# The last gate of a two-layer trunk: half of its K as seven block products instead of eight

## The chip, the cores and the metric

One core of a Trainium2 chip runs the whole program in one launch. The metric is device time in microseconds, of which the median over runs is given. The core has TensorE (PE, matmuls, with PEld its weight loads), VectorE (DVE), ScalarE (ACT), GpSimd (POOL) and SyncE (SP, which issues the DMA transfers of the kernel before). Each engine runs its own queue of instructions in order, and semaphores order them against each other.

## What is computed

A trunk of two layers over 512 tokens of 1024 channels in float32. Each layer has a token mixer, a squared-ReLU MLP, two layer norms, and at its end a gate:

```python
h = layer_norm(DEEPNORM_ALPHA * x + mix, ln_g[i, 0], ln_b[i, 0])
h = layer_norm(DEEPNORM_ALPHA * h + sq_relu_mlp(h, mlp_w1[i], mlp_w2[i]), ln_g[i, 1], ln_b[i, 1])
x = h + jax.nn.sigmoid(h @ ple_w_gate[i]) * (p[i] @ ple_w_proj[i])
```

The change is in the gate of the second layer, the last line at i = 1. There `h` is 512 x 1024, `ple_w_gate` 1024 x 1024, `p` 512 x 256 and `ple_w_proj` 256 x 1024; the result goes to the output.

## The kernel before

A float32 matrix is split into a high part (`hi`, rounded to the matmul's format) and a low part (`lo`, the remainder), and a product is three matmuls, high x high, high x low and low x high (`mm3`, L119). One matmul takes 128 rows of K, 128 tokens and 512 output columns. A weight arrives as a *unit* of 128 partitions x 1024 (two blocks of K by 512 columns, 512 KB): SP loads it into one of three `raw` buffers, ACT casts it to `whi` (L113), DVE subtracts to `wlo` (L116), in six buffers each.

The token dimension has four chunks of 128. The MLP's second matrix is applied in block products (`block_product`, L344), each of which replaces eight products of half blocks by seven with sums of blocks. Its weight sums are made by DVE in eight buffers `r` (`weight_sums`, L320). The last of them, in the order p1, p7, p6, p4, p5, p2, p3, ends with the layer norm: chunks 0 and 1 are normalised after p5, chunks 2 and 3 after p3 (`norm`, L283, `layer_norm`, L199), and each chunk of `acc` is transposed to serve as the stationary side of the gate (`transpose_split`, L231). A chunk has two groups of four transposes (q = 0 for the first half of the channels, q = 1 for the second); a group goes into a PSUM bank `pt`, ACT casts it (L242) and DVE subtracts (L243) into `h_s`.

The gate (L474 to L512) then runs over two halves `h` of the output columns and four chunks `c`: a projection of 6 matmuls (`proj`, L466) and a gate product of 24 matmuls over eight blocks of K (L493) into a PSUM bank `pj`; ACT takes the sigmoid (L496), DVE multiplies with the projection (L503) and adds `acc` (L506), and SP stores. In the first half all four projections come first, so that the transposes of chunks 0 and 1 can stand between them; those of chunks 2 and 3 stand inside the gate products of chunks 0 and 1. The very last projection is done in two halves of 256 columns behind the last gate product.

What sets the order: the program is scheduled by priorities when it is built. `tc.high_priority(offset=...)` moves instructions ahead by so many places (LEAD is 100, SOON 40); `behind(ins)` places one after a given instruction. From then on each engine's queue is fixed.

Of the kernel before, what the change touches and what calls it, by code (L numbers as in the profile page):

```python
# [15 lines left out]
P = 128  # L16
# [28 lines left out]
def trunk(ctx: ExitStack, tc, a):  # L45
# [73 lines left out]
    def mm3(out, sh, sl, mh, ml, start, stop, **kw):  # L119
        nc.tensor.matmul(out, sh, mh, start=start, stop=False, **kw)  # L120
        nc.tensor.matmul(out, sh, ml, start=False, stop=False, **kw)  # L121
        nc.tensor.matmul(out, sl, mh, start=False, stop=stop, **kw)  # L122

    class Split:

# [102 lines left out]
    def behind(ins):  # L228
        return tc.issue_after(ins.ins) if ins is not None else nullcontext()

    def transpose_split(src, dst, c, apart):  # L231

        sl = slice(c * P, (c + 1) * P)
        for q in range(2):
            pt = bank(psm, "pm") if apart and q else bank(pst, "pt")
            for j in range(4):
                k = 4 * q + j
                nc.tensor.transpose(pt[:, j * P : (j + 1) * P], src[:, k * P : (k + 1) * P], ident)  # L238
            v = pt.rearrange("p (j t) -> p j t", j=4)
            h = dst.hi[q][:, :, sl]  # L240
            with tc.high_priority(offset=LEAD if apart else SOON):
                nc.scalar.copy(h, v)  # L242
                turned_last[:] = [nc.vector.tensor_sub(dst.lo[q][:, :, sl], v, f32(h))]  # L243
            yield

    def out_part(units, n, xs, c, h, first, scale, last=False, sums=None):
# [33 lines left out]
                for c in range(NCH):  # L280
                    out_part(units, 4, xs, c, h, first, scale)

    def norm(i):  # L283
# [9 lines left out]
        return h_s, chunk, lambda c: transpose_split(acc[:, c, :], h_s, c, c == 3 and i % 2 == 0), sums  # L293

# [49 lines left out]
    def block_product(w, blk, lead, first, after=None, turns=None, sums=None, low=None):  # L344
# [41 lines left out]
        for f in (p1, p7, p6, p4, p5, p2, p3) if after else (p1, p2, p6, p7, p5, p4, p3):  # L386
# [4 lines left out]
                after(2), after(3)  # L391
            yield

    def mlp_and_gate(layer, h_s, last):

        w1, w2 = a[f"w1_{layer}"], a[f"w2_{layer}"]
# [34 lines left out]
        for g, period in enumerate(PERIODS):  # L431
            if g < 4:
                tiles = hidden(g)
            if g > 0:
                if g == 4:
                    h_s, after, turned, sums = norm(2 * layer + 1)
# [11 lines left out]
        x_n = None if last else Split(8)  # L448
        rows = None if last else [tmp("blk", [P, 2, 4, 256]) for _ in range(2)]
        late = []  # L450

        def turn(h, c):
# [10 lines left out]

        pps = {}

        def proj(c, pu, chunk=None, cs=slice(0, T)):  # L466

            ps = pps[c] = bank(*((psj, "pj") if c > 1 and pps else (psy, "py%d" % (c % 2))))
            sl = slice(c * P, (c + 1) * P) if chunk is None else slice(chunk * P, (chunk + 1) * P)
            for k in range(2):  # L470
                ks = slice(k * 512 + cs.start, k * 512 + cs.stop)
                mm3(ps[:, cs], p_s[0][:, k, sl], p_s[1][:, k, sl], pu[0][:, ks], pu[1][:, ks], k == 0, k == 1)

        for h in range(2):  # L474
            pu = unit(a[f"wp_{layer}"][h])
            gu = [unit(a[f"wg_{layer}"][4 * h + j]) for j in range(4)]
            for c in range(NCH):
                sl = slice(c * P, (c + 1) * P)
                if h == c == 0:
                    turns = turned(1)  # L480
                    for i in range(NCH):
                        proj(i, pu)
                        if i in (1, 2):
                            next(turns)
                end = last and h == 1 and c == NCH - 1
                if h == 1 and not end:
# [7 lines left out]
                    if turns and k in (2, 5):  # L494
                        next(turns)
                nc.scalar.activation(sg, pg, AF.Sigmoid)  # L496
                for i in range(2 if end else 1):
                    n = 256 if end else 512
                    cs = slice(i * n, (i + 1) * n)
                    if end:  # L500
                        proj(i, pu, c, cs)
                    pp = pps.pop(i if end else c)[:, cs]
                    nc.vector.tensor_mul(sg[:, cs], pp, sg[:, cs])  # L503
                    fs = slice(h * 512 + i * n, h * 512 + (i + 1) * n)
                    d = acc[:, c, fs]
                    nc.vector.tensor_add(d, sg[:, cs], d)  # L506
                    if last:
                        nc.sync.dma_start(a["out"][c * P : (c + 1) * P, fs], d)
                while late:
                    late.pop(0)()  # L510
                if not last:
                    late.append(lambda h=h, c=c: turn(h, c))  # L512
        return x_n, rows, late

    def values4(xs, rows, late):
# [791 lines left out]
```

## Time and profile before

| | |
|---|---|
| median of 3 runs | 1414.23 us (1414.07 to 1414.66) |
| the profiled execution | 1415.16 us |
| its span, first to last instruction | 1413.4 us |
| transposes behind the last block product start | 1350.97 us |
| last sigmoid of the gate starts | 1408.05 us |
| last operation of DVE starts | 1410.09 us |

A row of the timeline reads: start in us from the span's start, duration in us, engine, line of the kernel, operation, output<-inputs by the program's names, shapes, count, and in brackets how long the engine idled before it and what ended that. L numbers of profiles of before are lines of the kernel before. A row of a table of stretches has the stretch, its length, busy time (and instructions) of PE, PEld, DVE, ACT and POOL, the granted clock of TensorE as a share of full speed, the DMA engines' busy share and GB/s. The DMA rows end with the median time from issue to landing.

### The profile page before, as it was taken

To read this page: it belongs to the slowest core of one execution; us is meant where nothing else is said; L and a number is where in the kernel's file an instruction comes from. 1 tells how busy PE (TensorE), PEld (TensorE's weight loads), DVE (VectorE), ACT (ScalarE), POOL (GpSimd) and SP (SyncE) were. 2 spreads that over 40 slices of the span, in tenths; PEclk is the share of its full clock that TensorE was granted. 3 is DMA by queue.
4 is the path that set the end of the run, shared out by engine and by line. 5 is a ranking of instruction groups with operands and counts; after the bars stand their busy time and mean duration, and the time that the engine had idled before them with its cause. 6 is when DMAs were issued, how large, how long until landed. Compare 5 with 4: busy or idle time off the path is not lost.

```text
span 1413.4 us, 20324 instructions
## 1 busy us (share of the span) xinstructions
PE 1408.5 (100%) x8013; PEld 1170.9 (83%) x8013; DVE 1057.1 (75%) x1759; ACT 750.7 (53%) x1132; POOL 1.9 (0%) x12
## 2 busy tenths in 40 slices
PE   9999999999999999999999999999999999999998
PEld 7888888888988888888888888888888888888887
DVE  7989687698977668677986577678785857667873
ACT  6766465573354444545555547655555454544641
POOL 0000000000000000000000000000000000000000
PEclk9999999999999999999999999999999999999999
DMA  8433333234434444444621421222163444444231
GB/s 304 140 120 117 108 119 107 88 100 143 151 114 134 149 136 147 137 147 164 214 85 49 134 91 61 76 91 90 44 241 105 153 145 134 149 135 162 91 119 45
DMA packets 49391, 178.02 MB, mean 126 GB/s; under 512 B 5520, under 2 KB 6288, under 8 KB 49168
## 3 DMA queue, kind: packets, MB, share of 16 engines
q1 hardware_dynamic: 49296, 176.73, 37.9%
q8 instruction: 63, 1.03, 0.3%
q14 instruction: 32, 0.26, 0.1%
HBM read 174.54 MB, written 2.16 MB: 125 GB/s over the span
## 4 chain that ended last, share of the span: by engine, by line
PE 99%; DMA 0%; DVE 0%; issue 0%; DVEq 0%
PE pj L120 25%; PE pj L121 25%; PE pj L122 25%; PE py L120 5%; PE py L122 5%; PE py L121 5%; PE py L749 1%; PE pt L238 1%; PE py L1018 1%; PE pm L766 1%; PE pm L714 1%; PE py L1144 1%; PE pt L702 0%; PE py L1146 0%; PE py L1083 0%; PE py L675 0%
## 5 line engine op out<-in xcount | busy, mean ns | idle before, releaser
L113 ACT CAST whi<-raw 128x1024 fp32r<-128x1024 f32 x222 | 233.2, 1051 | 331.8 <-PE pj L121 241.8
L120 PE MATMUL pj<-b,whi 128*128 128x512 f32 (+1 forms) x990 | 378.7, 383 | 0.0
L122 PE MATMUL pj<-b,wlo 128*128 128x512 f32 (+1 forms) x990 | 376.7, 381 | 0.0
L121 PE MATMUL pj<-b,whi 128*128 128x512 f32 (+1 forms) x990 | 376.6, 381 | 0.0
L116 DVE TENSOR_TENSOR wlo<-raw,whi 128x1024 fp32r<-128x1024 f32 x222 | 270.2, 1221 | 136.9 <-ACT whi L113 134.6
L121 PEld LDWEIGHTS pj<-b,whi 128*128 128x128 f32 x990 | 186.3, 188 | 34.5 <-issue 0.9
L122 PEld LDWEIGHTS pj<-b,wlo 128*128 128x128 f32 x990 | 186.2, 188 | 34.5
L120 PEld LDWEIGHTS pj<-b,whi 128*128 128x128 f32 x990 | 186.1, 188 | 34.2
L122 PE MATMUL pj<-whi,b 128*128 128x512 f32 x544 | 213.4, 392 | 0.0
L120 PE MATMUL pj<-whi,b 128*128 128x512 f32 x536 | 213.0, 397 | 0.0
L121 PE MATMUL pj<-wlo,b 128*128 128x512 f32 x536 | 210.3, 392 | 0.0
L122 PEld LDWEIGHTS pj<-whi,b 128*128 128x128 f32 x544 | 102.2, 188 | 21.1
L120 PEld LDWEIGHTS pj<-whi,b 128*128 128x128 f32 x536 | 100.8, 188 | 20.3 <-ACT b L1165 0.3
L121 PEld LDWEIGHTS pj<-wlo,b 128*128 128x128 f32 x536 | 100.7, 188 | 19.8 <-issue 0.2
L113 ACT CAST whi<-r 128x1024 fp32r<-128x1024 f32 x72 | 75.7, 1053 | 67.7 <-PE pj L122 38.5
L116 DVE TENSOR_TENSOR wlo<-r,whi 128x1024 fp32r<-128x1024 f32 x72 | 87.7, 1220 | 21.6 <-ACT whi L113 20.9
L122 PE MATMUL py<-whi,b 128*128 128x512 f32 (+1 forms) x250 | 97.0, 388 | 0.0
L121 PE MATMUL py<-wlo,b 128*128 128x512 f32 x224 | 87.2, 389 | 0.0
L120 PE MATMUL py<-whi,b 128*128 128x512 f32 x224 | 87.1, 390 | 0.0
L643 DVE SCALAR_TENSOR_TENSOR cv<-pj,cst,cv 128x509 f32<-128x509 f32 (+2 forms) x66 | 48.9, 745 | 10.5 <-ACT cv L640 9.7
L122 PEld LDWEIGHTS py<-whi,b 128*128 128x128 f32 x250 | 46.9, 188 | 9.7
L120 PEld LDWEIGHTS py<-whi,b 128*128 128x128 f32 x224 | 42.0, 188 | 9.2 <-DVE sg L503 0.3
(316 smaller groups left out, 1848.0 us busy)
## 6 DMA issues: line engine op xcount, KB each, us to landing
raw<-in_w SPq DMA_DIRECT2D x112, 512.0 KB, 3.4
r<-in_w SPq DMA_DIRECT2D x64, 512.0 KB, 3.9
raw<-in_wssd SPq DMA_DIRECT2D x36, 512.0 KB, 4.0
a<-csd SPq DMA_DIRECT2D x16, 512.0 KB, 4.1
raw<-in_wso SPq DMA_DIRECT2D x16, 512.0 KB, 3.4
raw<-in_wg SPq DMA_DIRECT2D x16, 512.0 KB, 3.5
raw<-in_whq SPq DMA_DIRECT2D x16, 512.0 KB, 3.5
raw<-in_whvg SPq DMA_DIRECT2D x14, 512.0 KB, 3.4
```

Source lines behind the costliest of these rows:

```text
L113: nc.scalar.copy(hi[:, :n], f)
L116: nc.vector.tensor_sub(lo[:, :n], f, f32(hi[:, :n]))
L120: nc.tensor.matmul(out, sh, mh, start=start, stop=False, **kw)
L121: nc.tensor.matmul(out, sh, ml, start=False, stop=False, **kw)
L122: nc.tensor.matmul(out, sl, mh, start=False, stop=stop, **kw)
L238: nc.tensor.transpose(pt[:, j * P : (j + 1) * P], src[:, k * P : (k + 1) * P], ident)
L643: nc.vector.scalar_tensor_tensor(cv[:, d:], ps[:, : T - d], convw[:, i, k : k + 1], cv[:, d:], ALU.mult, ALU.add)
L714: nc.tensor.matmul(pst_[:, c * P : (c + 1) * P], btok[:, c, :], xw[:, c].rearrange("p h q -> p (h q)"), start=True, stop=True)
L749: mm = nc.tensor.matmul(yds[0][64 * r : 64 * r + 64, sl], xdt[:, 2 * c + r, :], m[:, r, sl], start=True, stop=True)
L766: mm = nc.tensor.matmul(yo[:, c * P : (c + 1) * P], pv[:, c - 1].rearrange("p h q -> p (h q)"), cm[:, c * P : (c + 1) * P], start=True, st ...
L1018: nc.tensor.matmul(pcs[r][bs, at : at + n], kk[r][:, ts], qs, start=True, stop=True)
L1144: nc.tensor.matmul(po[:, sl], scs[r][:, c, :], v(c, r), start=True, stop=c == 0)
```

## The change

The first half of the gate's K (512 channels, q = 0) is seen as a 2 x 2 block matrix A (256 tokens by 256 channels each) times a 2 x 2 block matrix B of weights (256 channels by 512 columns each): B11 = `wg[0]`, B21 = `wg[1]`, B12 = `wg[4]`, B22 = `wg[5]`. Eight products of blocks become seven:

- A11 B11 and A12 B21 as before,
- (A11 - A21) t3, with t3 = B12 + B22,
- (A21 - A22 - A11) t2, with t2 = t3 + B11,
- A22 t4, with t4 = t2 + B21,
- (A22 - A21) t1, with t1 = B12 + B11,
- (A11 + A22 - A21 - A12) B22.

The products are accumulated in PSUM, partly over each other; intermediate values are copied out by ACT into `cell`s and added by DVE. The second half of K (`rest`, 12 matmuls for each chunk and half) stays as it was. In the second half of the columns the sums come out negative, so its rests use negated weights (`negated`) and its sigmoid a scale of -1.

The sums t1 to t4 aren't made by DVE: POOL issues four loads of `wg[4]` into `r` buffers and seven transfers that add a block to what the buffer holds. The sums of A need the transposed chunks unsplit, so ACT copies each q = 0 group a second time (`keep`, into `kept`). Three projections of the second column half (chunks 2, 3 and 0) are made ahead of the products of sums and copied out to cells.

```diff
-    def transpose_split(src, dst, c, apart):
+    def transpose_split(src, dst, c, apart, keep=None):
...
-            pt = bank(psm, "pm") if apart and q else bank(pst, "pt")
+            pt = bank(psm, "pm") if (c == 3 if keep is not None else apart and q) else bank(pst, "pt")
...
-            with tc.high_priority(offset=LEAD if apart else SOON):
+            with tc.high_priority(offset=LEAD if apart or keep is not None else SOON):
                 nc.scalar.copy(h, v)
                 turned_last[:] = [nc.vector.tensor_sub(dst.lo[q][:, :, sl], v, f32(h))]
+                if keep is not None and q == 0:
+                    nc.scalar.copy(keep[:, c // 2, :, c % 2 * P : (c % 2 + 1) * P], v)
...
-            with tc.high_priority(offset=LEAD if c == 3 and i % 2 == 0 else SOON if c < 2 or i % 2 == 0 else 0):
+            with tc.high_priority(offset=LEAD if c == 3 and i % 2 == 0 else 0 if c > 1 and i == 1 else SOON):
                 layer_norm(i, c, gb, sums)
...
+    def last_gate(wp, wg, h_s, p_s, kept, turned):
+
+        t3, t1, t2, t4 = (tmp("r", [P, 1024]) for _ in range(4))
+        with tc.high_priority(offset=SOON):
+            for t in (t3, t1, t2, t4):
+                nc.gpsimd.dma_start(t, wg[4])
+            for t, n in ((t3, 5), (t1, 0), (t2, 5), (t4, 5), (t2, 0), (t4, 0), (t4, 1)):
+                nc.gpsimd.dma_start(t, wg[n], accum_op=ALU.add)
...
+        def negated(src):
+            with tc.high_priority(offset=LEAD):
+                raw = mk(raws, [P, 1024], "raw")
+                nc.sync.dma_start(raw, src)
+                hi = mk(whip, [P, 1024], "whi", F32R)
+                nc.scalar.activation(hi, raw, AF.Copy, scale=-1.0)
+                lo = mk(wlop, [P, 1024], "wlo", F32R)
+                nc.vector.scalar_tensor_tensor(lo, raw, -1.0, f32(hi), ALU.mult, ALU.subtract)
+            return hi, lo
...
+        def part(ps, x, w, u, start, stop=True):
+            for k in range(2):
+                ks = slice(k * 512, (k + 1) * 512)
+                mm3(ps, *x(k, u), w[0][:, ks], w[1][:, ks], start and k == 0, stop and k == 1, skip_group_check=True)
...
+        b11, b21 = unit(wg[0]), unit(wg[1])
+        us = [unit(wg[2]), unit(wg[3])]
+        t3 = split(t3)
+        turns = turned(1)
+        for c in range(NCH):
+            ps = bank(psj, "pj")
+            proj(ps, c, pu)
+            nc.scalar.copy(cell(c), ps)
+            if c in (1, 2):
+                next(turns)
+        x = [bank(psy, "py%d" % u) for u in range(2)]
+        for u in range(2):
+            part(x[u], direct(0, 0), b11, u, True)
+            nc.scalar.copy(cell(4 + u), x[u])
+
+        turns = [turned(2), turned(3)]
+        for u in range(2):
+            z = bank(psj, "pj")
+            next(turns[0])
+            part(z, direct(0, 1), b21, u, True, False)
+            next(turns[1])
+            rest(z, u, us, False)
+            nc.vector.tensor_add(cell(4 + u), z, cell(4 + u))
...
+        with tc.high_priority(offset=LEAD):
+            nc.vector.tensor_sub(a22, a22, a21)
+            nc.vector.tensor_sub(a21, a11, a21)
+            put(0, a21)
+            nc.vector.scalar_tensor_tensor(a11, a22, -1.0, a11, ALU.mult, ALU.subtract)
+            pin = put(1, a11)
+            put(2, a22)
+            nc.vector.scalar_tensor_tensor(a12, a12, -1.0, a11, ALU.mult, ALU.subtract)
+            put(3, a12)
...
+        for n, c in enumerate((2, 3, 0)):
+            ps = bank(psj, "pj")
+            proj(ps, c, pu)
+            nc.scalar.copy(cell(10 + n), ps)
+        for u in range(2):
+            final(u, 0, cell(4 + u), [(cell(u), whole)], pin)
+
+        t2, t4, t1 = split(t2), split(t4), split(t1)
+        y = [bank(psj, "pj") for _ in range(2)]
+        for u in range(2):
+            part(y[u], summed(0), t3, u, True)
+            nc.scalar.copy(cell(8 + u), y[u])
...
+        final(1, 1, x[1], [piece(psj, "pj", slice(0, 256)), piece(psm, "pm", slice(256, 512))])
```

In the changed kernel line numbers are higher; those of `transpose_split` and `layer_norm` that are named here (L113, L116, L215, L242, L243) stay, and L245 is the kept copy, L465 and L471 copies into cells, L486 the casts of A's sums, L491 and L492 the first two of these sums, L509 the copies of the moved projections, L401 the loads and L403 the adding transfers of POOL.

ACT's queue at the transposes of chunks 0 and 1, just behind the last block product. Before:

```order
L113 CAST whi_12003<-raw_12001 128x1024 [waits DMAHW3_49,PE_49]
L242 CAST b_1769_11420<-pt_11725 128x4x128 [waits PE_49]
L242 CAST b_1770_11421<-pt_11739 128x4x128 [waits PE_49]
L215 ACTIVATE sg_11757,lnsq_11755<-acc_99,lnmv_11753 128x512 [waits DVE_49,Activation_49]
L215 ACTIVATE sg_11759,lnsq_11755<-acc_99,lnmv_11753 128x512 [waits Activation_49]
L215 ACTIVATE sg_11771,lnsq_11769<-acc_99,lnmv_11767 128x512 [waits DVE_49,Activation_49]
L215 ACTIVATE sg_11773,lnsq_11769<-acc_99,lnmv_11767 128x512 [waits Activation_49]
L242 CAST b_1769_11420<-pt_11825 128x4x128 [waits PE_49]
```

And in the changed kernel:

```order
L113 CAST whi_11834<-r_11783 128x1024 [waits DMASW1_49,PE_49]
L242 CAST b_1770_11421<-pt_11726 128x4x128 [waits PE_49]
L245 COPY blk_11416<-pt_11726 128x4x128 [waits DVE_49]
L242 CAST b_1771_11422<-pt_11741 128x4x128 [waits PE_49]
L465 COPY b_1858_11800<-pj_11838 128x512
L465 COPY b_1858_11800<-pj_11846 128x512
L215 ACTIVATE sg_11759,lnsq_11757<-acc_99,lnmv_11755 128x512 [waits DVE_49,Activation_49]
L242 CAST b_1770_11421<-pt_11854 128x4x128 [waits PE_49]
L215 ACTIVATE sg_11761,lnsq_11757<-acc_99,lnmv_11755 128x512 [waits Activation_49]
L215 ACTIVATE sg_11773,lnsq_11771<-acc_99,lnmv_11769 128x512 [waits DVE_49,Activation_49]
L245 COPY blk_11416<-pt_11854 128x4x128 [waits DVE_49]
```

The weight split ahead of the casts is now that of t3 and waits for POOL's transfer (DMASW); a kept copy stands behind the first cast of each chunk, and copies of projections stand between.

ACT's queue a little later, between the transposes of chunk 1 and those of chunks 2 and 3, in the changed kernel (before, there stood four casts L242, the sigmoid's table load and sigmoids):

```order
L465 COPY b_1858_11800<-pj_11862 128x512
L113 CAST whi_12023<-r_11785 128x1024 [waits DMASW0_49]
L504 CAST a_11984<-raw_11983 128x1024 [waits DMAHW3_49,DVE_49]
L113 CAST whi_12027<-r_11786 128x1024 [waits DMASW2_49,PE_49]
L242 CAST b_1770_11421<-pt_11902 128x4x128 [waits PE_49]
L465 COPY b_1858_11800<-pj_11877 128x512
L471 COPY b_1859_11801<-py_1885_11885 128x512
L242 CAST b_1770_11421<-pm_11916 128x4x128 [waits PE_49]
L471 COPY b_1859_11801<-py_1886_11886 128x512
L245 COPY blk_11416<-pt_11902 128x4x128 [waits DVE_49]
L113 CAST whi_12031<-r_11784 128x1024 [waits DMASW4_49,PE_49]
L245 COPY blk_11416<-pm_11916 128x4x128 [waits DVE_49]
```

The splits of t2 (`r_11785`), of the second projection weights and of t4 (`r_11786`) stand ahead of the casts of chunks 2 and 3; that of t1 (`r_11784`) stands behind.

POOL's queue, which before ended with the clearing of mixer buffers, in the changed kernel:

```order
L401 DMA r_11783<-in_wg 128x1024 [waits DMAHW1_49,DMAHW6_49,DMAHW0_49,DMAHW7_49,DVE_49,PE_49]
L403 DMA r_11783<-in_wg 128x1024 [waits DMASW0_49]
L401 DMA r_11784<-in_wg 128x1024 [waits DVE_49]
L401 DMA r_11785<-in_wg 128x1024 [waits DVE_49]
L403 DMA r_11784<-in_wg 128x1024 [waits DMASW2_49]
L401 DMA r_11786<-in_wg 128x1024 [waits DVE_49]
L403 DMA r_11785<-in_wg 128x1024 [waits DMASW3_49]
L403 DMA r_11786<-in_wg 128x1024 [waits DMASW5_49]
L403 DMA r_11785<-in_wg 128x1024 [waits DMASW6_49]
L403 DMA r_11786<-in_wg 128x1024 [waits DMASW7_49,DMASW1_49]
L403 DMA r_11786<-in_wg 128x1024 [waits DMASW1_49]
```

t3 is `r_11783`, t1 `r_11784`, t2 `r_11785`, t4 `r_11786`. Loads wait for DVE to be done with the buffer's contents of the last block product, adding transfers for the landing of the one before in the same buffer.

More of the change, by code (lines that the diff above doesn't have):

```diff
@@ L435, in mlp_and_gate @@
                 if g == 4:
-                    h_s, after, turned, sums = norm(2 * layer + 1)
+                    kept = tmp("blk", [P, 2, 4, 256]) if last else None
+                    h_s, after, turned, sums = norm(2 * layer + 1, kept)
                     p_s = (mk(w4, [P, 2, T], "a", F32R), mk(w4, [P, 2, T], "b", F32R))
@@ L446, in mlp_and_gate @@
                 next(tiles if op == "T" else products)
-        x_n = None if last else Split(8)
-        rows = None if last else [tmp("blk", [P, 2, 4, 256]) for _ in range(2)]
+        if last:
+            return last_gate(a[f"wp_{layer}"], a[f"wg_{layer}"], h_s, p_s, kept, turned)
+        x_n = Split(8)
+        rows = [tmp("blk", [P, 2, 4, 256]) for _ in range(2)]
         late = []
@@ L484, in mlp_and_gate @@
                             next(turns)
-                end = last and h == 1 and c == NCH - 1
-                if h == 1 and not end:
+                if h == 1:
                     proj(c, pu)
@@ L496, in mlp_and_gate @@
                 nc.scalar.activation(sg, pg, AF.Sigmoid)
[L497 to L508, printed above, removed]
+                nc.vector.tensor_mul(sg, pps.pop(c), sg)
+                d = acc[:, c, h * 512 : (h + 1) * 512]
+                nc.vector.tensor_add(d, sg, d)
                 while late:
                     late.pop(0)()
-                if not last:
-                    late.append(lambda h=h, c=c: turn(h, c))
+                late.append(lambda h=h, c=c: turn(h, c))
         return x_n, rows, late
```

88 lines of the change are left out of this document (81 added, 7 removed).

## The prediction, made before the changed kernel was run

> **What bounds the kernel now.** I read the page first, then the tail (from 1300 us on) in the timelines of PE, ACT and DVE, then the table of stretches and the DMA rows.
>
> ```profile
> span 1413.4 us, 20324 instructions
> ...
> PE 1408.5 (100%) x8013; PEld 1170.9 (83%) x8013; DVE 1057.1 (75%) x1759; ACT 750.7 (53%) x1132; POOL 1.9 (0%) x12
> ...
> PE 99%; DMA 0%; DVE 0%; issue 0%; DVEq 0%
> ```
>
> TensorE is busy in all of the span and the chain that ended last is 99% PE. So the kernel is a queue of matmuls, and a change is worth the matmuls it takes from that queue less the waits that it puts into it. What a matmul costs there is not the 0.38 to 0.39 us that the page gives as the duration of one, since they overlap. It is the step between starts, read from two sigmoids that each wait for the end of a chunk:
>
> ```profile
> 1389.01 0.60 ACT L496 ACTIVATE sg<-pj 128x512 f32<-128x512 f32 x1 [6.20 <-PE pj L122]
> 1395.81 0.60 ACT L496 ACTIVATE sg<-pj 128x512 f32<-128x512 f32 x1 [6.20 <-PE pj L122]
> ```
>
> Between them PE does 24 gate and 6 projection matmuls: 6.80 / 30 = 0.2267 us each. The same rows show that ACT idles for 6.2 us of every 6.8 in the second half of the gate, so instructions added there have cover. The first half is another matter:
>
> ```profile
> 1310.00:1318.00 8.00, 8.00 (x36) 6.47 (x35) 7.79 (x12) 5.37 (x8) 0.00 (x0) 1.00 0.21 65
> 1318.00:1326.00 8.00, 8.00 (x36) 6.57 (x36) 7.87 (x12) 5.88 (x6) 0.00 (x0) 1.00 0.01 4
> 1326.00:1334.00 8.00, 8.00 (x37) 6.60 (x36) 6.90 (x9) 2.63 (x3) 0.00 (x0) 1.00 0.52 156
> 1342.00:1350.00 8.00, 8.00 (x37) 6.63 (x36) 8.00 (x16) 4.11 (x9) 0.00 (x0) 1.00 0.57 178
> 1350.00:1358.00 8.00, 8.00 (x42) 6.63 (x42) 7.56 (x14) 5.13 (x11) 0.00 (x0) 1.00 0.55 173
> 1358.00:1366.00 8.00, 8.00 (x40) 6.54 (x40) 6.91 (x11) 5.03 (x10) 0.00 (x0) 1.00 0.32 110
> ```
>
> Columns: stretch, its length, then busy time of PE, PEld, DVE, ACT and POOL, PE's clock, DMA share, GB/s. DVE has nothing free from 1342 to 1350 and little until 1366, just where the change adds sums, copies and drains. PE never idles in these rows, so no wait is there to be removed.
>
> **The change part by part.** *PE.* In the last gate 8 groups of 24 matmuls (192) become 14 parts of 6 and 8 rests of 12 (180). Projections stay at seven of 6 and one in two halves, transposes at eight groups of four. Everything ahead of the layer's last block product is row for row the same. So 12 x 0.2267 = **2.72 us go**, and nothing more can: that is 0.19%.
>
> *Place 1, transposes of chunks 0 and 1.* The second group of transposes takes the bank `pt` of the first. So far one ACT cast and one DVE subtraction had to be through with it; now the kept copy (L245) too, and it waits for DVE.
>
> ```profile
> 1350.97 0.60 PE L238 MATMUL pt<-cst,acc 128*128 128x128 f32 x4
> 1351.32 0.48 PE L120 MATMUL pj<-whi,a 128*128 128x512 f32 x1
> 1351.63 0.39 PE L121 MATMUL pj<-wlo,a 128*128 128x512 f32 x1
> ...
> 1352.18 0.58 ACT L242 CAST b<-pt 128x512 fp32r<-128x512 f32 x1
> ...
> 1349.43 2.48 DVE L224 SCALAR_TENSOR_TENSOR acc<-acc,lnrs,b 128x1024 f32<-128x1024 f32 x2
> 1351.83 1.22 DVE L116 TENSOR_TENSOR wlo<-raw,whi 128x1024 fp32r<-128x1024 f32 x1
> 1352.96 0.69 DVE L370 CUSTOM_DVE_ANT_0 acc<-py,acc 128x512 f32<-128x512 f32 x1
> 1353.57 0.69 DVE L243 TENSOR_TENSOR b<-pt,b 128x512 fp32r<-128x512 f32 x1
> ```
>
> In the new order DVE's subtraction stands ahead of the drain: 1352.96 + 0.69 = 1353.65; the copy, at the 0.58 of the cast, ends at 1354.25. PE gets to the second group after 13 matmuls: a group of four and the restart cost 0.44 (0.35 from the first to the second row, and 0.31 - 0.23 more at the third), so 1350.97 + 0.44 + 13 x 0.2267 = 1354.35. It fits by 0.1 us. Walked on in the same way, the groups at 1356.8 and 1360.2 fit by 0.1 to 0.2. Cost 0, but with no cover left.
>
> *Place 2, transposes of chunks 2 and 3.* Between the fourth cast and the kept copy of chunk 2, ACT now has a projection copy, three splits of 1024 columns, and then five casts and copies of 512.
>
> ```profile
> 1354.63 0.60 PE L238 MATMUL pt<-cst,acc 128*128 128x128 f32 x4
> ...
> 1355.26 0.59 ACT L242 CAST b<-pt 128x512 fp32r<-128x512 f32 x1 [2.50 <-PE pt L238]
> 1355.74 0.72 ACT L215 ACTIVATE sg<-acc,lnmv 128x512 f32<-128x512 f32 x1
> ...
> 1359.43 1.04 ACT L113 CAST whi<-raw 128x1024 fp32r<-128x1024 f32 x1
> ...
> 1313.80 0.69 DVE L312 TENSOR_TENSOR a<-a 128x512 f32<-128x512 f32 x1
> 1314.41 0.69 DVE L306 TENSOR_TENSOR blk<-b,blk 128x512 fp32r<-128x512 f32 x1
> ```
>
> A group's cast starts 0.63 us after the group (1354.63 to 1355.26) and occupies ACT for 0.5 (to 1355.74). PE reaches the fourth group at 1360.2, so its cast starts at 1360.85, and with it (0.5), a square root (0.15), the projection copy (0.5), three splits (1.0 each) and five casts and copies (0.5 each) ACT is taken until 1367.5; the kept copy ends at 1368.1. PE arrives at the first q1 group after three groups and 28 matmuls: 1360.2 + 3 x 0.44 + 28 x 0.2267 = 1367.9. **Wait 0.3 us**, with the signal.
>
> Late next are the sums of A. ACT still has the split of t1 and one kept copy ahead of the cast of that group, which so ends at 1370.2; then DVE has two subtractions L243, L491 and L492 at steps of 0.6 (1313.80 to 1314.41) and is through at 1372.8. ACT's first two casts of sums follow, and behind them in its queue the copy of the first moved projection, until 1374.4. The third moved projection needs that copy's bank at 1367.9 + 0.3 + 2 x 0.44 + 21 x 0.2267 = 1373.85: **wait 0.5 us.** The three projections hide the rest: without them the products of sums would be asked for 18 x 0.2267 = 4.1 us earlier, and that much would be idle.
>
> *Waits with little margin.* Five waits of PE in this walk have 0.2 us or less. One slip among them costs its own length and gives the others slack, so they don't add. Bounds 0 and 2 us (a 1024-column DVE instruction of 1.22 and a cast of 0.59 out of place); the walked margins are nearest to the low end, I take **0.3 us**.
>
> *POOL's eleven transfers.* No row of before has a POOL transfer or an adding one. The nearest are SP's of the same size:
>
> ```profile
> r<-in_w SPq DMA_DIRECT2D x64, 512.0 KB, 3.9
> ...
> raw<-in_wp SPq DMA_DIRECT2D x4, 512.0 KB, 3.8
> ...
> b<-in_xw SPq DMA_DIRECT2D x2, 512.0 KB, 8.1
> ...
> 1304.13 1.22 DVE L116 TENSOR_TENSOR wlo<-r,whi 128x1024 fp32r<-128x1024 f32 x1
> 1315.01 1.22 DVE L116 TENSOR_TENSOR wlo<-r,whi 128x1024 fp32r<-128x1024 f32 x1
> ```
>
> The four buffers come free as DVE ends its splits of t3 and t2 of the last block product: 1305.35 the first, 1316.2 the last. Through POOL's queue the sum t4, last to be ready, needs six landings in a row. At 3.9 us each (none adding up slower than a load) it is there by 1331, at 8.1 us (the loads at the start, when many run at once) by 1354. ACT comes to t4's split at about 1364.1 by the walk above. So they are hidden up to 58.7 / 6 = 9.8 us a landing: **cost 0**, low bound 0 since PE waits for no weight today, high bound the rival below. What covers them: POOL does nothing else, and the DMA share is 0.21 and 0.01 in the rows from 1310 to 1326.
>
> [...]
>
> *The rest.* The later copies and adds and the two negated splits fall after 1376, under ACT's 6.2 us of idle. The end (last sigmoid, two half projections, four DVE operations, the last store) keeps its form: 0.
>
> Sum: -2.72 + 0.3 + 0.5 + 0.3 = -1.6 us. The profiled run took 1415.16 us with a span of 1413.4, 0.93 above the median of 1414.23. So the profile should show a span near 1411.8, and the median **1412.6 us**.
>
> **The rivals.**
>
> 1. *Slower: the adding transfers are late.* ACT's split of t4 stands ahead of the casts of chunk 2 and 3's transposes, so whatever t4 is late, PE waits for. It decides from 9.8 us a landing and eats the gain from 10.1. At 11 us: 1305.35 + 66 = 1371.4, 7.3 late, 1412.6 + 7.3 = **1419.9**. [...] Chance 0.10.
>
> [...]
>
> 2. *The transfers crowd others.* From 1326 SP's loads take 0.52 to 0.57 of the DMA engines. Loads of `raw` that overlap take 4.6 where a lone one takes 3.3:
>
> ```profile
> DMA to landing us min/median/max: 3.3/3.5/4.6
> ...
> 1346.17 1.06 ACT L113 CAST whi<-raw 128x1024 fp32r<-128x1024 f32 x1 [0.23 <-DMA raw<-in_wg]
> ```
>
> One load is already 0.23 late for ACT. Its cast, the square roots behind it and DVE's L224 (through at 1350.7) lead to the transposes at 1350.97: some 0.5 us of slack. Loads 2 us longer cost about 1.5; or DVE loses as much to POOL in its full stretches. **1414.1**, no change. Against it: at 3.9 us a landing the transfers end by 1331. Chance 0.20.
>
> 3. *ACT and DVE are the bound from 1350 to 1376.* If each of their added rows costs 0.1 us more than the row I took, some 25 in a row put 2.5 us on PE: **1415.1**. DVE at 8.00 of 8.00 speaks for it; that the same forms have rows speaks against. Chance 0.10.
>
> 4. *No wait at all:* 1414.23 - 2.72 = **1411.5**. The walked waits are 0.3 and 0.5 us, within what such a walk can miss. Chance 0.12.
>
> **How the numbers follow.** The forecast has 0.48, with a range of its own from 1411.9 to 1413.4 (gains of 2.3 to 0.8 us). A measurement of this kernel tells about 0.2%, 2.8 us, from no change: faster is under 1411.4, slower over 1417.1. The twelve matmuls are worth less than that, so faster needs all of rival 4 and a little luck: 0.06. Slower is rival 1 (0.10), the far ends of 2 and 3 (0.04) and mishaps of the walk (0.02): 0.16. The rest, 0.78, is the same. The range takes rivals 2 to 4 in and leaves most of 1 out: 1411.3 to 1417.0.
>
> **What would show it.** In the profile after: PE with 12 fewer 512-column matmuls and a gap of 0.2 to 0.6 us ahead of a transpose group about 17 us behind the last block product and ahead of a projection some 6 us later. POOL's transfers landing within 5 us each, the last before 1340; ACT's splits of `r` in the gate with no DMA as releaser. A splits row that waits for a DMA of `r` for over 1 us proves rival 1; `raw` loads of 5 us and more, or DVE rows longer than 1.28, prove rival 2; several PE gaps released by ACT from 1350 on prove rival 3. The forecast is wrong if the span shrinks by more than 2.7 us or if PE's waits after 1350 come to over 2.5.

## The result, and the profile after

| | median us | runs | lowest to highest | against the kernel before |
|---|---|---|---|---|
| before | 1414.28 | 12 | 1413.97 to 1415.04 | |
| after | 1418.39 | 12 | 1415.88 to 1419.93 | 1.0029 (95%: 1.0020 to 1.0038) |

The change makes the kernel slower by 4.1 us. The forecast was 1412.6, so the answer lies 5.8 us from it and 1.4 us outside the range. The profiled execution took 1417.95 us, near the median. First the page after the change, the rows that answer to those of before:

```profile
span 1416.2 us, 20365 instructions
...
PE 1408.1 (99%) x8001; PEld 1170.3 (83%) x8001; DVE 1070.8 (76%) x1778; ACT 764.3 (54%) x1156; POOL 10.3 (1%) x23
...
q1 hardware_dynamic: 49152, 176.20, 36.7%
q0 software_dynamic: 1584, 5.77, 1.9%
...
PE 96%; DVE 1%; DMA 1%; ACT 1%; issue 0%; ACTq 0%; DVEq 0%
```

PE did run 12 matmuls fewer (8001 for 8013), yet the span grew by 2.8 us, and the chain that was 99% PE now holds some DVE, DMA and ACT: PE waited for somebody. `q0` is POOL's transfers, which the kernel before did not have. Where it waited, the table of stretches says (columns as before: busy PE, PEld, DVE, ACT, POOL, PE's clock, DMA share, GB/s):

```profile
1318.00:1326.00 8.00, 8.00 (x37) 6.60 (x36) 7.87 (x10) 5.10 (x5) 1.84 (x3) 1.00 0.99 216
1326.00:1334.00 8.00, 8.00 (x37) 6.63 (x36) 6.06 (x9) 2.11 (x2) 1.74 (x2) 1.00 0.90 183
1334.00:1342.00 8.00, 8.00 (x37) 6.61 (x36) 4.49 (x9) 3.33 (x5) 0.39 (x1) 1.00 1.03 312
1342.00:1350.00 8.00, 8.00 (x37) 6.53 (x35) 6.95 (x11) 5.84 (x12) 0.48 (x1) 1.00 0.81 236
1350.00:1358.00 8.00, 5.17 (x16) 4.02 (x15) 8.00 (x13) 3.30 (x6) 0.00 (x0) 0.64 0.54 194
1358.00:1366.00 8.00, 8.00 (x41) 6.53 (x40) 3.56 (x10) 5.76 (x15) 0.00 (x0) 0.93 0.01 3
```

Read it from two sides. In the fifth row PE is busy for 5.17 of 8 us, with 16 matmuls for the usual 37, and its clock is 0.64: a wait, and slow matmuls behind it. In the first four rows the DMA engines are full (0.99, 0.90, 1.03, 0.81, where before they stood at 0.01, 0.52, 0.50 and 0.57), and in the second and third DVE and ACT have lost work (DVE 6.06 and 4.49, before 6.90 and 5.60). The row of before for the third stretch, the only one of the first four not shown yet:

```profile
1334.00:1342.00 8.00, 8.00 (x37) 6.64 (x36) 5.60 (x10) 5.00 (x8) 0.00 (x0) 1.00 0.50 174
```

The loads came late, then the vector work, then PE. The timeline of PE shows the wait itself (start, duration, engine, line, tiles, and in brackets the idle time before it with what ended it):

```profile
1349.89 0.39 PE L122 MATMUL py<-whi,blk 128*128 128x512 f32 x1
1353.11 1.11 PE L238 MATMUL pt<-cst,acc 128*128 128x128 f32 x4 [2.83 <-DVE acc L224]
1353.87 0.77 PE L120 MATMUL pj<-whi,a 128*128 128x512 f32 x1
1354.44 0.63 PE L121 MATMUL pj<-wlo,a 128*128 128x512 f32 x1
...
1359.14 0.40 PE L120 MATMUL pj<-whi,a 128*128 128x512 f32 x1
```

The first row is the last matmul of the last block product. The first transposes of chunk 0 start 3.22 us behind it, 3.0 more than a step, because the layer norm's last operation (L224) is late. Then twelve steps take 1359.14 - 1353.87 = 5.27 us instead of 12 x 0.2267 = 2.72: **2.5 us more at half the clock**. The group of transposes itself takes 0.76 us for 0.35 (1353.11 to 1353.87), 0.4 more. With the gap of the third moved projection (0.4, below) the sum is -2.72 + 3.0 + 0.4 + 2.5 + 0.4 = +3.6. The spans differ by +2.8, because in this execution the last block product ended 0.84 us earlier than in the profile before (its last matmul starts at 1349.89 for 1350.73).

What made L224 late stands in the timelines of ACT and DVE of the same kernel, and in the DMA issues from 1326 to 1346:

```profile
1335.32 1.05 ACT L113 CAST whi<-raw 128x1024 fp32r<-128x1024 f32 x1 [5.70 <-DMA raw<-in_w]
...
1348.81 1.05 ACT L113 CAST whi<-raw 128x1024 fp32r<-128x1024 f32 x1 [0.68 <-DMA raw<-in_wg]
1349.77 0.48 ACT L219 ACTIVATE lnsd<-lnmv,cst 128x1 f32<-128x1 f32 x2
...
1348.63 2.49 DVE L116 TENSOR_TENSOR wlo<-raw,whi 128x1024 fp32r<-128x1024 f32 x2
...
1351.77 2.48 DVE L224 SCALAR_TENSOR_TENSOR acc<-acc,lnrs,b 128x1024 f32<-128x1024 f32 x2
```

```profile
...
r<-in_wg POOLq DMA_DIRECT2D x3, 512.0 KB, 8.6
raw<-in_w SPq DMA_DIRECT2D x2, 512.0 KB, 7.8
raw<-in_wp SPq DMA_DIRECT2D x1, 512.0 KB, 9.7
```

In the kernel before ACT doesn't wait for `raw<-in_w` there, and the second view reads:

```profile
raw<-in_w SPq DMA_DIRECT2D x2, 512.0 KB, 3.4
raw<-in_wp SPq DMA_DIRECT2D x1, 512.0 KB, 4.1
```

The last two weights of the last block product (`raw<-in_w`) take 7.8 us for 3.4, the first of the gate 9.7 for 4.1. There are three `raw` buffers, so a late load is split late, frees its buffer late and delays the load that takes this buffer next. At the end of this ring a gate weight lands late and ACT casts it at 1348.81. Two things then wait for that cast: the square roots of the layer norm (L219), which are through at 1350.25, and DVE's split of the same weight (L116), which is through at 1351.1. The split is the later one. Behind it in DVE's queue stand the reciprocal (L221), the drain of a PSUM bank into `acc` (L372) and then L224. The sums themselves were early: the last of POOL's transfers landed at 1347.1 (issued at 1341.61, 5.5 us), and ACT split that tile at about 1369 without waiting.

### The profile page after: what moved, and what is told of

Its sections match the earlier page's. It is cut to its first block, busy times and chain, and to the rows that moved or that the text cites. A ratio compares the mean times of both kernels' runs of the same rounds, so it can differ in the third digit from the quotient of the medians.

```text
span 1416.2 us, 20365 instructions
## 1 busy us (share of the span) xinstructions
PE 1408.1 (99%) x8001; PEld 1170.3 (83%) x8001; DVE 1070.8 (76%) x1778; ACT 764.3 (54%) x1156; POOL 10.3 (1%) x23
## 3 DMA queue, kind: packets, MB, share of 16 engines
q1 hardware_dynamic: 49152, 176.20, 36.7%
q8 instruction: 63, 1.03, 0.3%
## 4 chain that ended last, share of the span: by engine, by line
PE 96%; DVE 1%; DMA 1%; ACT 1%; issue 0%; ACTq 0%; DVEq 0%
PE pj L120 24%; PE pj L121 24%; PE pj L122 24%; PE py L120 5%; PE py L121 5%; PE py L122 5%; PE py L900 1%; PE pt L238 1%; PE py L1169 1%; PE pm L917 1%; PE pm L865 1%; DVE wlo L116 1%; DMA raw<-in_w 1%; PE py L1295 1%; PE pt L853 0%; PE py L1297 0%
## 5 line engine op out<-in xcount | busy, mean ns | idle before, releaser
L113 ACT CAST whi<-raw 128x1024 fp32r<-128x1024 f32 x218 | 229.0, 1051 | 332.5 <-PE pj L121 242.3
L116 DVE TENSOR_TENSOR wlo<-raw,whi 128x1024 fp32r<-128x1024 f32 x218 | 265.6, 1222 | 143.6 <-ACT whi L113 140.0
L122 PE MATMUL pj<-whi,b 128*128 128x512 f32 x520 | 205.0, 394 | 0.0
L120 PE MATMUL pj<-whi,b 128*128 128x512 f32 x508 | 202.1, 398 | 0.0
L121 PE MATMUL pj<-wlo,b 128*128 128x512 f32 x508 | 199.1, 392 | 0.0
L113 ACT CAST whi<-r 128x1024 fp32r<-128x1024 f32 x76 | 80.0, 1054 | 67.7 <-PE pj L122 38.2
L122 PEld LDWEIGHTS pj<-whi,b 128*128 128x128 f32 x520 | 98.3, 189 | 20.4
L120 PEld LDWEIGHTS pj<-whi,b 128*128 128x128 f32 x508 | 95.5, 188 | 19.0 <-ACT b L1316 0.3
L121 PEld LDWEIGHTS pj<-wlo,b 128*128 128x128 f32 x508 | 95.5, 188 | 18.8 <-issue 0.2
L116 DVE TENSOR_TENSOR wlo<-r,whi 128x1024 fp32r<-128x1024 f32 x76 | 92.6, 1221 | 23.3 <-ACT whi L113 22.7
L122 PE MATMUL py<-whi,b 128*128 128x512 f32 x260 | 101.3, 390 | 0.0
L121 PE MATMUL py<-wlo,b 128*128 128x512 f32 x248 | 96.5, 389 | 0.0
L120 PE MATMUL py<-whi,b 128*128 128x512 f32 x248 | 96.4, 390 | 0.0
L122 PEld LDWEIGHTS py<-whi,b 128*128 128x128 f32 x260 | 48.8, 188 | 10.2
L120 PEld LDWEIGHTS py<-whi,b 128*128 128x128 f32 x248 | 46.6, 188 | 10.1 <-DVE sg L658 0.3
```

The costliest lines, as they stand in the source:

```text
L113: nc.scalar.copy(hi[:, :n], f)
L116: nc.vector.tensor_sub(lo[:, :n], f, f32(hi[:, :n]))
L122: return nc.tensor.matmul(out, sl, mh, start=False, stop=stop, **kw)
```

## The experiments

The two medians of a row were measured together on one chip, so experiments are compared by their difference from their own kernel before; that of the change is +4.1 us. The intervals are about 1.3 us to either side, wider for 3 and 4, so differences under that are not shown.

| | median us | lowest to highest | before | ratio (95%) |
|---|---|---|---|---|
| 1 loads alone, no adding | 1412.49 | 1412.09 to 1413.35 | 1414.87 | 0.9984 (0.9975 to 0.9993) |
| 2 adding made plain loads | 1413.38 | 1412.28 to 1416.57 | 1414.87 | 0.9993 (0.9984 to 1.0002) |
| 3 before, with the eleven transfers | 1421.69 | 1419.12 to 1422.95 | 1414.87 | 1.0047 (1.0031 to 1.0062) |
| 4 PE kept busy in the gap | 1419.71 | 1418.41 to 1420.80 | 1414.74 | 1.0035 (1.0021 to 1.0049) |
| 5 four transfers held back | 1414.91 | 1413.57 to 1418.18 | 1414.87 | 1.0003 (0.9994 to 1.0012) |
| 6 four adding transfers for seven | 1413.21 | 1412.02 to 1415.20 | 1414.74 | 0.9990 (0.9981 to 0.9999) |
| 7 as 6, projections put back | 1416.19 | 1414.89 to 1419.09 | 1414.74 | 1.0012 (1.0003 to 1.0021) |
| 8 as 6, t1 held back | 1412.34 | 1411.97 to 1413.09 | 1414.79 | 0.9983 (0.9974 to 0.9992) |

In experiments 1 and 2 the sums of weights are left out, so their results are not those of the trunk. In experiments 1, 2, 3, 5, 6 and 8 the instructions of PE, ACT, DVE and SP stand in the same order as in the kernel they start from; only POOL's queue differs.

**Experiment 1: the four loads without the adding.**

```
-            for t, n in ((t3, 5), (t1, 0), (t2, 5), (t4, 5), (t2, 0), (t4, 0), (t4, 1)):
-                nc.gpsimd.dma_start(t, wg[n], accum_op=ALU.add)
```

> The changed kernel with its four POOL loads, but without the seven adding transfers (the sums of weights are left out, each of the four buffers holds one plain quarter). Order of every other engine unchanged. Crowding theory (POOL's transfers share the DMA engines with the late loads of w2 and wp, these come 4 to 5.6 us late, the layer norm behind them leaves PE idle for 2.8 us and the clock is then granted at half for some 6 us): the four loads are through before 1327, the w2 loads land in about 3.5 us, no step of PE over 1 us at the end of the block products, no slow matmuls behind it, about 1412.3 us (1411.5 to 1413.2). Rival, the new copies, casts and sums on ScalarE and VectorE are the loss: nothing changes for them, the time stays at 1417 to 1419.

The late loads, the gap and the slow clock are all gone, and all the rest of the change is still there. So the new copies, casts and sums on ACT and DVE are not the loss. From 1300 us on only one step of PE stands out in its timeline:

```profile
1374.43 0.50 PE L120 MATMUL pj<-a,a 128*128 128x512 f32 x1 [0.22 <-ACT b L507]
```

It is the third moved projection, whose first matmul starts 0.60 us behind the last one of the second (1373.83), 0.37 more than a step. -2.72 + 0.37 = -2.35 us, and the measured difference is 1412.49 - 1414.87 = -2.38.

**Experiment 2: the seven adding transfers as plain loads.** In the code, `accum_op=ALU.add` is taken out.

> The changed kernel with the seven adding transfers made plain loads of the same bytes into the same buffers (so the sums of weights are left out); eleven transfers in the same places of POOL's queue, other engines unchanged. If the bytes and their place crowd the loads: w2 and wp loads still 6 us and more, gap of 2 to 3 us and slow clock behind it, 1416.5 to 1418.5. If adding is what takes the DMA engines' time: transfers of POOL fall from 5.4 to 9 us towards 4 to 5, the chain ends before 1335, the w2 loads are less than 2 us late, and the time is 1412 to 1414.

The share of the DMA engines that POOL's transfers take, of experiment 2's page (the queue, its packets, MB, and time on 16 engines as a share of the span):

```profile
q0 software_dynamic: 1584, 5.77, 1.1%
```

The same bytes took 1.9% after the change. One plain transfer is 0.011 x 1411.7 / 11 = 1.4 us of all 16 engines; the eleven of the change are 0.019 x 1416.2 = 26.9 us, of which four plain ones take 5.6, so **an adding one takes 21.3 / 7 = 3.0 us, twice a plain one** (experiments 6 and 8, with four of each and a share of 1.3%, give 3.2). An SP load, by `q1` of the page after, takes 0.367 x 1416.2 us for 176.20 MB, or 1.55 us for 512 KB (0.524 MB).

Both expectations hold in part. The time falls by most of the loss, as the adding theory had it, but the w2 loads still take 5.4 and 6.3 us, and the gap is there at a fifth of its size, in PE's timeline (the profiled execution took 1413.46 us; others took up to 1416.57):

```profile
1351.30 0.66 PE L238 MATMUL pt<-cst,acc 128*128 128x128 f32 x4 [0.60 <-DVE acc L224]
```

The matmuls behind it run at full clock. So it is traffic, the time of the DMA engines, that does the harm, and adding is twice the traffic.

**Experiment 3: the kernel before, and the eleven transfers.** At the start of its last gate stand the six lines of the change that issue them, into the same `r` buffers.

> The kernel before, with nothing but the eleven POOL transfers of the change put in, into the same four buffers, which nothing reads (result as before). Crowding theory: the same late w2 and wp loads, gap ahead of the first transposes of 2 to 3 us and slow matmuls behind it, 1414.3 + 3 to 6 = 1417 to 1420 us. Rival, the loss lies in the new last gate: these transfers cost nothing, 1414.3 us (within 0.5).

1421.69 - 1414.87 = +6.8 us, more than the 3 to 6 expected, with no other part of the change in it. It matches what the adding transfers cost inside the change: +4.1 against the -2.4 of experiment 1, or 6.5. PE's timeline:

```profile
1350.22 0.39 PE L122 MATMUL py<-whi,blk 128*128 128x512 f32 x1
1354.16 1.12 PE L238 MATMUL pt<-cst,acc 128*128 128x128 f32 x4 [3.55 <-DVE acc L224]
1354.93 0.78 PE L120 MATMUL pj<-whi,a 128*128 128x512 f32 x1
1355.50 0.63 PE L121 MATMUL pj<-wlo,a 128*128 128x512 f32 x1
```

The same place, the same releaser, the same slow matmuls. That settles the cause: the transfers alone, with no reader, make the loss.

**Experiment 4: PE kept busy in the gap.** The lines stand behind the last matmul of the last block product; `v` is a tile that is long there, the rounded half of p, which the projections read.

```
+                        pt, v = bank(psm, "pm"), fill_src[0]
+                        for _ in range(12):
+                            with tc.high_priority(offset=100), behind(ins):
+                                ins = nc.tensor.matmul(pt[:, :512], v[:, 0, :P], v[:, 1, :512], start=True, stop=True)
```

> The changed kernel with twelve needless 512-column matmuls on TensorE between the last block product and the first transposes (into a bank that is free; the result as before), so that TensorE works through most of the idle 2.8 us there. VectorE's and ScalarE's rows ahead of the first transposes are the same, some behind them change places. Theory that the idle time itself brings the clock down: the transposes still wait for the layer norm, until about 1353, but the matmuls behind them step at 0.23 us and not at 0.43, clock 1.000 in nearly all runs, and the median falls by the 2.4 us to about 1416 (1415.3 to 1417.5, the changed places included). Rival, the clock falls for another reason (the DMA traffic, or the place in the program): steps of 0.43 us as before the edit, 1417.5 to 1419.

```profile
1350.49 0.39 PE L122 MATMUL py<-whi,blk 128*128 128x512 f32 x1
1350.71 2.88 PE L374 MATMUL pm<-a 128*128 128x512 f32 x12
1354.10 0.66 PE L239 MATMUL pt<-cst,acc 128*128 128x128 f32 x4 [0.51 <-DVE acc L224]
1354.52 0.49 PE L120 MATMUL pj<-whi,a 128*128 128x512 f32 x1
1354.84 0.40 PE L121 MATMUL pj<-wlo,a 128*128 128x512 f32 x1
...
1360.01 0.66 PE L239 MATMUL pt<-cst,acc 128*128 128x128 f32 x4 [2.47 <-ACT blk L246]
```

In the profiled execution the transposes start 3.61 us behind the last block product, even later than after the change (3.22), but PE was idle for only 0.51 us of that, and the matmuls behind them are 0.40 long and step at 0.23 us. So the slow clock came from the idle time and not from the traffic or the place. The median did not fall, though, as was expected (+5.0 us, against +4.1), since a new wait of 2.47 us came in at the second transposes. The profiled execution is the fastest of four (1418.41) and the only one with a mean granted clock of 1.000; the others read 0.999, and where their clock fell was not traced. Whose wait that is, ACT's timeline says:

```profile
1359.37 0.59 ACT L246 COPY blk<-pt 128x512 f32<-128x512 f32 x1 [3.98 <-DVE b L244]
```

It is the kept copy (L245 of the change). The filling moved DVE's subtraction (L244 here, L243 of the change) behind a split and two drains, the copy waits for that subtraction, and the transposes wait for the copy's bank. This is the wait that the prediction called "cost 0, but with no cover left"; with a few rows of DVE in another order it cost all that the clock gave.

**Experiment 5: the sums as they are, four transfers held back.**

```
+        sums(((t3, 4), (t4, 4), (t3, 5), (t4, 5), (t2, 4), (t4, 0), (t4, 1)))
...
+            held = nc.gpsimd.tensor_copy(t1[:, :1], f32(us[1][0])[:, :1])
+        with behind(held):
+            sums(((t1, 4), (t2, 5), (t1, 0), (t2, 0)))
```

> The changed kernel with all its work, but POOL's queue in another order: seven transfers (t3 and t4 whole, the load of t2) ahead, then a one-column copy on POOL that waits for the cast of the last of the four weight units in front of the last gate (about 1347), and behind it the other four (load of t1, and three adding ones). Order of all other engines unchanged. Crowding theory: the w2 and wp loads are at most 1 to 2 us late, no gap over 1 us and no slow clock at the end of the block products; t2 is complete near 1360 and needed near 1362; 1412.0 to 1413.5 us, so faster than both. If t2 is late, 1 to 4 us more with a wait of ScalarE on that transfer. Rival, the loss is in ScalarE's and VectorE's added work: 1417 to 1419 as before the edit.

4.1 us better than the change (+0.04 us against its kernel before), but no faster than that kernel: the 1412.0 to 1413.5 us expected were missed. Two waits are left, one at each end, in PE's timeline:

```profile
1351.60 0.66 PE L238 MATMUL pt<-cst,acc 128*128 128x128 f32 x4 [1.26 <-DVE acc L224]
...
1370.17 0.66 PE L238 MATMUL pt<-cst,acc 128*128 128x128 f32 x4 [1.06 <-ACT blk L245]
```

The first is the old one: the transfers ahead ended only at 1340, since an adding one beside SP's loads took 9.5 us (issued at 1330.66). The second is new, and ACT's timeline shows its start:

```profile
1364.26 1.05 ACT L113 CAST whi<-r 128x1024 fp32r<-128x1024 f32 x1 [1.18 <-DMA r<-in_wg]
```

t2 landed 1.18 us late for its split, ACT's casts and kept copies queue behind that split, and PE waits for their bank. Moving four of the eleven transfers was not enough: the seven ahead still met SP's loads, and those behind came late.

**Experiment 6: less traffic for the same sums.** t1 to t4 hold the same sums; each later tile takes an earlier one instead of adding its parts anew.

```
+            for t, n in ((t3, 4), (t2, 0), (t4, 1), (t1, 0)):
+                nc.gpsimd.dma_start(t, wg[n])
+            for t, s in ((t3, wg[5]), (t2, t3), (t4, t2), (t1, wg[4])):
+                nc.gpsimd.dma_start(t, s, accum_op=ALU.add)
```

> The changed kernel with its sums made from each other: four plain POOL loads (t3, t2, t4, t1) and four adding transfers in place of seven: a quarter onto t3, the tile t3 onto t2, the tile t2 onto t4, a quarter onto t1. Same four sums, other engines' order unchanged. Crowding theory: at about 3.7 us a load and 5.3 an adding transfer they are through by about 1326, the w2 loads take 3.4 us again, no gap over 0.7 us at the end, 1412.0 to 1413.2 us, so faster than both and within 0.3 us of the run without any adding. Rival, any adding transfer next to the loads is enough: two to four of them are still under way at 1328, gap of 1 to 3 us, 1414 to 1417.

Faster than before by 1.5 us, and 5.6 below the change. But the last transfer, the adding one onto t1, was issued at 1323.92 and took 7.6 us, to 1331.5, into the w2 loads (4.7 and 5.7 us), and the runs still spread from 1412.0 to 1415.2.

**Experiment 7: the three moved projections put back** behind the products of sums, with the sums as in experiment 6.

> The kernel with four adding transfers, with the three moved projections put back behind the products of sums. By the walk of the prediction the sums of A are then asked for 4.1 us earlier, while VectorE and ScalarE have them no earlier: a gap of 3 to 4.5 us ahead of the first product of sums, 3 to 4 us more than with the projections in front (about 1416), or 5 to 7 more if the clock falls behind the gap. Rival, the sums are ready by then: no gap, 1412 to 1413.

1416.19 against 1413.21: 3.0 us more. That is the low end of the 3 to 4 us expected without a fall of the clock, but the clock did fall in the profiled execution, for which 5 to 7 were expected: the gap is 2.10 us and not 3 to 4.5, and the nine matmuls behind it take 3.76 us for 2.04. That execution took 1417.34 us, 1.2 above the median, and has a gap of 0.70 at the first transposes besides. PE's timeline and stretch:

```profile
1371.63 0.40 PE L122 MATMUL pj<-whi,b 128*128 128x512 f32 x1
1374.13 0.72 PE L120 MATMUL pj<-whi,b 128*128 128x512 f32 x1 [2.10 <-ACT b L486]
1374.65 0.63 PE L121 MATMUL pj<-wlo,b 128*128 128x512 f32 x1
```

```profile
1374.00:1382.00 8.00, 7.87 (x28) 6.33 (x28) 6.65 (x11) 5.34 (x9) 0.00 (x0) 0.79 0.00 2
```

PE waits for the casts of A's sums, and the clock falls again. The DMA engines do nothing here (share 0.00), so it is not traffic that slows it.

**Experiment 8: and t1 held back**, load and adding, behind the one-column copy of experiment 5; t1 is the sum that is needed last.

> The kernel with four adding transfers made from each other, and of its eight the two of t1 (load and adding), the sum that is needed last, held back behind a one-column copy on POOL that waits for the cast of the last weight unit in front of the last gate (about 1347). All work is done; the order of the other engines is unchanged. Crowding theory: the six transfers that stay ahead are through by about 1326, the w2 loads land in 3.3 to 4.2 us instead of 4.7 to 5.7, no step of PE over 0.65 us behind the block products in any common run, the spread of the runs shrinks towards that of the run without adding (1412.1 to 1413.4), median 1412.3 to 1412.9: the best version. If t1 is late for its split (it has to land by about 1366), a wait of ScalarE on it and 1 to 3 us more. Rival, the spread has another cause than crowding: as before this edit, 1412 to 1415 with a median of 1413.2.

1412.34 us, 2.45 below the kernel before and 6.6 below the change, with the spread of experiment 1. The median is 0.9 us below that of experiment 6, which the intervals don't separate; the slowest execution is 1413.09 for 1415.20. The DMA issues from 1326 to 1346:

```profile
...
raw<-in_w SPq DMA_DIRECT2D x2, 512.0 KB, 3.3
raw<-in_wp SPq DMA_DIRECT2D x1, 512.0 KB, 4.3
```

The w2 loads are back at 3.3 us. PE goes from the last block product into the transposes without a break:

```profile
1350.33 0.40 PE L122 MATMUL py<-whi,blk 128*128 128x512 f32 x1
1350.56 0.60 PE L238 MATMUL pt<-cst,acc 128*128 128x128 f32 x4
```

All the work of the change is in this kernel, so its idea is worth the 2.45 us. The traffic of its sums cost 6.6 and made +4.1 of it.

## Why the prediction was wrong

*The twelve matmuls, -2.72: right.* Experiments 1 and 8 end at -2.38 and -2.45, which is -2.72 and the one wait that is left.

*The third moved projection, 0.5: right,* 0.37 in experiment 1, with the releaser that the walk named (the copy behind the casts).

*Place 1, 0 with no cover left: right.* No gap there in experiments 1, 6 and 8, and 2.47 us of it as soon as experiment 4 changed a few rows of DVE.

*Place 2, 0.3, and the thin margins, 0.3: too high.* Both came to 0 where the loads are on time. That ACT's delays do end in this bank experiment 5 shows, 1.06 us.

*The projections as cover, "4.1 us earlier, and that much would be idle": right in kind, 2.1 us in size,* and in experiment 7 the clock falls behind that gap besides.

*"POOL's eleven transfers ... cost 0": the step that failed.* It asked whether the transfers are late for their own reader, and they were not: rival 1 fell, the last one landed more than 20 us ahead of its split. What it didn't ask is whether they fit. The hole that it named as cover runs from the first free `r` buffer at 1305.35 to the w2 loads, issued from 1327.37 on: 22 us. Even eleven transfers at SP's 1.55 us of all engines would have filled 17 us of it, and in truth they took 26.9. Where the sum has 0, the first transposes have 3.0 us of waiting and 2.9 of slow clock behind it. (The time that the prediction gives for t4 at 3.9 us a landing is its own slip: 1305.35 + 6 x 3.9 = 1328.8, not 1331. It changes nothing.) In "What would show it", landings "within 5 us each, the last before 1340" became 3.8 to 8.9 us and 1347.

*Rival 2 had the mechanism and the wrong size.* It named the victims (`raw` loads, the cast at 1346.17 ahead of the square roots, L224, the transposes) and the sign `raw` loads of 5 us and more, and both came (on DVE, the split of the late weight ended behind the square roots and so was the last link). But it said 2 us longer, cost 1.5; they were 4.4 to 5.6 us longer, and the gap was 3.0. Its argument against itself, that at 3.9 us a landing the transfers end by 1331, rested on SP's plain load as the nearest row of an adding transfer, whose landings after the change are 5.4 to 8.9 us. At 2 us longer the price would have been lower still: experiment 2, with w2 loads 2 to 3 us longer, has a gap of 0.60.

*The missing term: the clock.* No rival priced what a wait of PE does to the matmuls behind it. It is 2.9 of the 5.9 us at that place (2.5 of the twelve matmuls, 0.4 of the transposes), and the runs of the change show it too: the two in which the mean granted clock reads 1.000 took 1415.88 and 1416.79, the ten at 0.998 or 0.999 took 1417.68 to 1419.93.

*Rival 3 (ACT and DVE the bound) fell* with experiment 1; the splits of DVE (L116) last 1222 ns before and 1224 after.

## What to carry to other kernels

Cost a transfer that is hidden for its own reader by the engine time that it takes from others: DMA time needed (share of the queue in the page, over its count) against the hole it is to fill (here 26.9 us against 22), and then the deadlines of the loads on the far side of that hole. Give a PE wait of 2 to 3 us a range up to twice its length (after the change 3.0 us of waiting had 2.9 of slow clock behind it), since the matmuls behind it may run at half the clock (they did behind 2.10, 2.83 and 3.55 us here, and did not behind 2.47). When a scheme brings traffic of its own, cut the traffic first (a sum made from another sum) and place what is left by the order of need; here that turned +4.1 us into -2.45.

## What the hardware showed that was not expected

*Adding costs the DMA engines twice a plain transfer* (3.0 against 1.4 us of all 16 for 512 KB) and lands in 5.0 to 6.2 us in experiment 8, a plain POOL load in 3.6 to 4.5 in experiment 1. Beside POOL's transfers SP's w2 loads slow down: they land in 7.8 us after the change and in 3.4 before, where POOL issues none.

*PE's clock falls behind an idle time of 2.10 us (experiment 7), 2.83 (after) or 3.55 (experiment 3) and does not fall behind 2.47 (experiment 4) or 1.26 (experiment 5).* So the length of the idle time alone doesn't decide. What does decide shows in these traces: the clock changes only at the ends of equal intervals of 3.41 us. After the change it is halved from 1352.31 to 1359.14 us, two intervals, and the next change of that trace, at 1417.16, just behind its span, lies 17 intervals on; in experiment 7 it is halved from 1374.25 to 1377.66, one; in experiment 4 it changes at 1416.24 only, and counting back from there gives its intervals. The stretches are these intervals, of after, of experiment 7 and of experiment 4:

```profile
1348.90:1352.31 3.41, 1.38 (x7) 0.80 (x5) 3.36 (x7) 3.22 (x5) 0.00 (x0) 1.00 0.43 167
1352.31:1355.72 3.41, 2.61 (x8) 2.23 (x9) 3.41 (x4) 0.59 (x1) 0.00 (x0) 0.50 0.50 169
1355.72:1359.14 3.42, 3.42 (x10) 2.63 (x8) 2.61 (x6) 0.59 (x1) 0.00 (x0) 0.50 0.43 153
...
1370.84:1374.25 3.41, 1.31 (x8) 0.81 (x8) 3.25 (x5) 1.86 (x4) 0.00 (x0) 1.00 0.48 156
1374.25:1377.66 3.41, 3.41 (x9) 2.65 (x10) 3.41 (x7) 0.97 (x2) 0.00 (x0) 0.50 0.01 2
...
1354.80:1358.21 3.41, 2.74 (x12) 1.88 (x10) 3.41 (x6) 0.58 (x1) 0.00 (x0) 1.00 0.42 156
1358.21:1361.63 3.42, 1.62 (x9) 1.43 (x10) 1.59 (x7) 2.26 (x6) 0.00 (x0) 1.00 0.23 91
```

Behind an interval in which PE was busy for 1.38 or 1.31 us (1.02 in experiment 3, where the clock is 0.69 from 1350 to 1358), the next one runs at half the clock; behind 1.62 (experiment 4) or at least 2.15 (experiment 5, 3.41 less its wait of 1.26) it does not. The wait of 2.47 us did no harm because the end of an interval cut it, 0.67 us before and 1.80 behind. At half the clock a full interval (3.42 us of work after the change, 3.41 in experiment 7) brings the clock back and one with 2.61 us of work (after the change) does not. In these traces the limit lies between 1.38 and 1.62 us of work; no run here narrows it further, or tests it in another kernel. So whether a wait of this size costs double is partly luck, and that fits the spread of the runs of the change: by an estimate from two intervals, 6.83 x 0.5 / 1416, the mean clock of an execution should read 0.998, with one 0.999 and with none 1.000, and these are the three values that its runs have. Nor need an interval be idle throughout: 1.38 us of work in one did not keep the clock.
